# A two-block network on one core: a change to its norms and to one copy in an expert stage

## The chip, the cores and the metric

The kernel runs on one core of one Trainium2 chip, as one launch. The metric is the device time of that launch in microseconds (us). The median of three runs of the kernel before is 4241.9 us; the runs lie from 4215.21 to 4246.16 us.

The engines are named as the profile names them: PE is TensorE (matmuls), PEld its weight loads, DVE is VectorE, ACT is ScalarE, POOL is GpSimd, and SP issues most of the transfers.

## The reference, cut to what matters

A first block (two layers, each a feed-forward net, a mixer of three recurrences, and a second feed-forward net) works on 256 tokens of width 1024. A second block (two layers, attention and an expert stage each) works on the same 256 tokens and on 256 context tokens. What the change touches is the norms, and the expert stage of the second block's first layer.

```python
def rmsnorm(x, w):
    xf = x.astype(jnp.float32)
    y = xf * lax.rsqrt(jnp.mean(xf * xf, axis=-1, keepdims=True) + EPS)
    return (y * w.astype(jnp.float32)).astype(x.dtype)
...
def chunk(args):
    hc, ic, gc = args
    ue = u[ic]
    ve = v[ic]
    act = jax.nn.gelu(jnp.einsum('td,ted->te', hc, ue), approximate=False)
    return jnp.einsum('te,ted->td', gc * act, ve)
```

The kernel computes the expert stage densely: all 16384 experts for every token, times a gate that is zero for the experts that were not chosen.

## The kernel before, in words

**Layout.** Activations stand transposed: channels on the 128 partitions, tokens along the row, so x is a tile of 128 x 8 x 256 (eight channel blocks of 256 tokens). Everything is float32. A matmul of full precision is three matmuls (`mm3`, L242) on operands split into a high and a low part: `split` (L214) takes the high part with an ACT copy (L221) and the low part with a subtraction on DVE (L224), part of it on POOL (L226). `mm` (L239, L240) records every matmul, so all of PE's rows bear L240.

**The order of the work.** No order is written out by hand. The program is traced once, and a planner lays out each engine's queue from a modelled timeline: of the instructions that are ready there, the one traced earliest goes first. On the chip each engine then works through its queue in that order. Tiles of one tag share a fixed number of buffers, and a new tile waits until an old one has been read for the last time.

**The norm.** `quick_rstd` (L299) is the quick form. It squares the eight channel blocks into eight tiles of the tag `g_n`, five on ACT (L308) and three on DVE (L306; blocks 2, 3 and 6). The tag has 4 buffers in the two mixers and in the last expert stage, 5 in the attention of the second block, and 6 in the two closing norms and at the expert stage of the context tokens (`self.gb`, key `n`). `rstd_of` (L288) then sums over the partitions on PE: for every tile of squares, two matmuls with the squares as weights and a column of ones as the moving operand, all into one bank. The trace shows each of them as two matmuls of one column (`pj<-ones,g_n`, or `act<-ones`, `s<-ones`), so 32 for a norm. `rsqrt` (L249) makes the reciprocal root of the 128 x 2 sums on DVE, by an integer guess and three Newton steps, and `spread` (L268) puts it on all partitions with two matmuls by the identity (`pj<-ccom,rsy`). The next work (L328 or L1588) multiplies x with it. Eight norms go this way: one in each mixer, the two closing norms (`scaled_norm`, L1583), one in the attention of x in each layer of the second block, one on the context tokens ahead of the first expert stage, and one ahead of the last expert stage. Eight other norms use `rstd` (L275), which adds its squares on DVE (L284) and hands one tile to `rstd_of`. `rsqrt` has 26 calls in all, 10 of them from norms of heads (`head_rstd`, L312, and L826) on 128 x 8 values.

**The expert stage of the first layer** (`peer_both`, L1528). Groups 0 to 8 run for the context tokens alone (256 tokens, `experts` with `first`), while the gates of x are still being made (`gates`, L1408: DVE makes `g_e` and `g_o`, PE multiplies them into the bank `r`, ACT copies that into `rst` (L1432), and a transfer writes `rst` to the DRAM tensor `gd`). The results stand in four PSUM banks, `acc`. Then groups 9 to 31 run for x and the context tokens together (512 tokens): `hidden` (L1449) loads weights of `u` (into `raw` and `rawx`), splits them (ACT L221) and multiplies; `gated` (L1466) loads the gates (`eG<-gd`, L1469) and multiplies on DVE (L1473), then splits (`eah`, `eal`); `down` (L1478) multiplies by `v` into the banks `acc`, and DVE adds them into the SBUF tile `ef` (L1500). Between the two, ACT copies the four banks of the context tokens into the right half of `ef` (L1556). The first `down` of the 512-token stage needs those banks.

Of the kernel before, what the change touches and what calls it, by code (L numbers as in the profile page):

```python
# [14 lines left out]
I32 = mybir.dt.int32  # L15
# [4 lines left out]
OP = mybir.AluOpType  # L20
# [88 lines left out]
class Net:  # L109
# [42 lines left out]
    def t(self, shape, tag, bufs=1, dt=F32, pool=None):  # L152
        return (pool or self.ph).tile(shape, dt, tag=tag, name=tag, bufs=bufs)
# [95 lines left out]
    def rsqrt(self, ss, n, scale=1.0):  # L249

        nc = self.nc
        c = ss.free_size()
        t = lambda tag, dt=F32: self.t([128, 16], "rs" + tag, 2, dt)[:, 0:c]
        x, xh, a, y = t("x"), t("h"), t("a"), t("y", I32)
        nc.vector.tensor_scalar(x, ss, 1.0 / n, EPS, OP.mult, OP.add)
        nc.vector.tensor_scalar(y, x.bitcast(I32), 1, None, OP.logical_shift_right)
        nc.vector.tensor_scalar_mul(xh, x, -0.5)
        nc.vector.tensor_scalar(y, y, -1.0, float(0x5F3759DF), OP.mult, OP.add)
        y = y.bitcast(F32)
        for _ in range(3):  # L260
            nc.vector.tensor_tensor(a, y, y, OP.mult)
            nc.vector.tensor_tensor(a, a, xh, OP.mult)
            nc.vector.scalar_tensor_tensor(y, a, 1.5, y, OP.add, OP.mult)
        if scale != 1.0:
            nc.vector.tensor_scalar_mul(y, y, scale)
        return y
# [32 lines left out]
    def quick_rstd(self, x):  # L299

        nc = self.nc
        sqs = []
        for k in range(8):
            sqs.append(self.g([128, 256]))
            if k in (2, 3, 6):
                nc.vector.tensor_tensor(sqs[k], x[:, k], x[:, k], OP.mult)  # L306
            else:
                nc.scalar.activation(sqs[k], x[:, k], AF.Square)  # L308
        self.pooled = 2
        return self.rstd_of(sqs)  # L310

    def head_rstd(self, sqs, n, scale, tag):  # L312

# [1118 lines left out]
                    nc.scalar.copy(st.rearrange("p i t -> p t i")[:, t0:t0 + 4], ps)  # L1432
            nc.scalar.dma_start(gd[base + c], st.rearrange("p i t -> p (i t)"))

    def experts(self, h, grps, u_d, v_d, gd, f=None, quiet=()):

        nc = self.nc
        T = h[0].shape[2]  # L1440
        nt = T // 32
        pairs = 512 // T
        gi = pairs
        acc = None
        if T == 256:
            acc = [self.bank((128, 2, 256), "acc") for _ in range(4)]
        acts, G = {}, {}

        def hidden(grp):  # L1449
            self.lead = 0 if T == 512 else LEAD  # L1450
            acts[grp] = []
            for b in range(4):
                if b % 2 == 0:
                    raw = self.raw(u_d[grp * 2 + b // 2])
                W = self.wsplit(raw[:, b % 2 * 1024:(b % 2 + 1) * 1024], [128, 1024])
                if b % pairs == 0:
                    ps = self.bank((128, pairs, T), "act")
                for k in range(8):
                    self.mm3(ps[:, b % pairs], [q[:, k * 128:(k + 1) * 128] for q in W], [q[:, k] for q in h],
                             k == 0 and b % pairs == 0, k == 7 and b % pairs == pairs - 1)  # L1460
                if b % pairs == pairs - 1:
                    a = self.t([128, pairs, nt, 32], "ea", self.na, pool=self.ap_)
                    nc.scalar.activation(a.rearrange("p b c t -> p b (c t)"), ps, AF.Gelu)
                    acts[grp].append(a)

        def gated(grp):  # L1466
            if grp % gi == 0:
                G[0] = self.t([128, nt, 4 * gi, 32], "eG", 2)
                nc.sync.dma_start(G[0], gd.rearrange("c p (i t) -> p c i t", t=32)[:, :, grp * 4:(grp + gi) * 4])  # L1469
            out = []  # L1470
            for n, a in enumerate(acts.pop(grp)):
                for q in range(pairs):
                    nc.vector.tensor_tensor(a[:, q], a[:, q], G[0][:, :, grp % gi * 4 + n * pairs + q], OP.mult)  # L1473
                A = self.split(a.rearrange("p b c t -> p b (c t)"), [128, pairs, T], "ea", 4)
                out += [[z[:, q] for z in A] for q in range(pairs)]
            return out

        def down(grp):  # L1478
            As = gated(grp)
            self.lead = 0 if T == 512 else LEAD  # L1480
            for half in range(2):
                raw = self.raw(v_d[grp * 2 + half])
                if T == 512:
                    banks = [self.bank((128, 512), "acc") for _ in range(4)]
                for b in range(4):
                    if b % 2 == 0:
                        W = self.wsplit(raw[:, b // 2 * 1024:(b // 2 + 1) * 1024], [128, 1024])
                    for m in range(4):
                        o = b % 2 * 512 + m * 128
                        w = [q[:, o:o + 128] for q in W]  # L1490
                        if T == 512:
                            self.mm3(banks[m], w, As[b], b == 0, b == 3)
                        else:
                            mm = half * 4 + m
                            self.mm3(acc[mm // 2][:, mm % 2], w, As[b], grp == grps[0] and b == 0 and mm % 2 == 0,
                                     grp == grps[-1] and b == 3 and mm % 2 == 1)
                if T == 512:
                    for m in range(4):
                        o = f[:, half * 4 + m]
                        nc.vector.tensor_tensor(o, o, banks[m], OP.add)  # L1500

        lag = self.na * pairs // 4 - 1
        for grp in grps:
            self.share = 0 if grp in quiet else 256
            hidden(grp)
            if grp - lag in grps:
                self.xp = self.xp or self.spare
                down(grp - lag)
            yield
        for grp in grps[-lag:] if lag else ():  # L1510
            down(grp)
        self.share, self.lead = 0, LEAD
        return acc
# [14 lines left out]
    def peer_both(self, l, x, ctx, wq_d, keys_d, u_d, v_d, gd, beside):  # L1528

        first, rest = range(0, NFIRST), range(NFIRST, 32)  # L1530
        with self.tc.tile_pool(name="eh", bufs=1, reuse_waits="tile") as hp, self.psum("ex", act=2, acc=4):
            ps, pb = self.ps, self.pb

            def run(gen):
                self.ps, self.pb, self.al, self.ph = ps, pb, {}, hp
                try:
                    while True:
                        yield next(gen)
                except StopIteration as e:
                    self.acc = e.value  # L1540

            self.ap_, self.na, self.ph = hp, 4, hp
            h = (self.t([128, 8, 512], "pH", 1, F32R), self.t([128, 8, 512], "pL", 1, F32R))
            hx, hc = [[q[:, :, j * 256:(j + 1) * 256] for q in h] for j in range(2)]
            self.gb, self.al = dict(n=6), dict(pj="act")
            self.mnorm(ctx, l, 3, 1, hc)
            self.al = {}
            gen = self.experts(hc, first, u_d, v_d, gd[8:16], quiet=range(4, NFIRST))
            next(gen)
            self.route(self.queries(x, l, 0, 2, hx), wq_d, keys_d, gd, 0)  # L1550
            list(run(gen))
            with self.roomy(), self.tc.tile_pool(name="ef", bufs=1, reuse_waits="tile") as fp:
                f = self.t([128, 8, 512], "ef", pool=fp)
                self.nc.gpsimd.memset(f[:, :, 0:256], 0.0)
                for m in range(4):
                    self.nc.scalar.copy(f[:, 2 * m:2 * m + 2, 256:512], self.acc[m])  # L1556
                list(run(self.experts(h, rest, u_d, v_d, gd, f)))
                self.residual(ctx, l, 5, 1, [f[:, 2 * m:2 * m + 2, 256:512] for m in range(4)])
                next(beside)
                for i, _ in enumerate(run(self.experts(hx, first, u_d, v_d, gd[0:8]))):  # L1560
                    if i == 2:
                        list(beside)
                        self.ps, self.pb, self.al, self.ph = ps, pb, {}, hp
                self.residual(x, l, 5, 0, [f[:, 2 * m:2 * m + 2, 0:256] for m in range(4)])
                self.residual(x, l, 5, 0, self.acc)
# [230 lines left out]
```

## Time and profile before

| | |
|---|---|
| median of 3 runs | 4241.9 us (4215.21 to 4246.16) |
| the profiled execution's own time | 4208.75 us |
| its span | 4206.7 us, 76811 instructions |
| mean granted clock of PE | 0.983 |
| PE busy | 4071.0 us (97%) |
| DVE busy | 2822.1 us (67%) |
| ACT busy | 1943.9 us (46%) |
| POOL busy | 1324.3 us (31%) |
| DMA | 727.42 MB, mean 173 GB/s |

The profiled execution is one run of its own: its time is 33 us below the median of the three, and 2 us of it lie outside its span. Every duration read from the trace belongs to it. In a row of the timeline the columns are the start, the duration, the engine, the line, the operation, the tiles written and read, their shapes and the count, and in brackets the idle time of the engine before it with what ended it. A row with a count above one has merged neighbours, and its duration is that of them all.

### The profile page before, as it was taken

Reading aid. Unit: us, or ns where it says so; the run is one execution under the profiler, and the core shown is the slowest. Engines: PE = TensorE matmul, PEld = TensorE weight load, DVE = VectorE, ACT = ScalarE, POOL = GpSimd, SP = SyncE. Lnnn points to the kernel's source line nnn. Section 1 sums busy time; section 2 is a strip of 40 time slices with the busy share of each in tenths; the row PEclk is TensorE's granted clock in tenths of the full one; section 3 lists DMA queues with packets and bytes.
Section 4 is the critical chain, followed back from the end, with each engine's and each line's share of the span. In section 5 each row is a group of like instructions: output and inputs, shape, how many; then the busy total and the mean of one; then the engine's idle time right before and its main releaser. Section 6 shows DMA issues by size and latency. Waiting matters only on the chain.

```text
span 4206.7 us, 76811 instructions
## 1 busy us (share of the span) xinstructions
PE 4071.0 (97%) x31290; PEld 3768.6 (90%) x31290; DVE 2822.1 (67%) x5280; ACT 1943.9 (46%) x2711; POOL 1324.3 (31%) x1239
## 2 busy tenths in 40 slices
PE   8999999999999999999999999999999899899999
PEld 8988999998979987999788888888998699799999
DVE  5686757786869957999444444444656789865555
ACT  4462555545536644566322323232444646544443
POOL 4542444454402201400222222222354130015554
PEclk9999999999999989999999999999999999999999
DMA  5545644545465542466533333433464236676654
GB/s 215 175 175 201 234 172 161 192 152 193 146 226 211 211 169 106 150 219 222 170 120 120 120 120 120 130 111 130 154 212 160 75 139 225 240 276 211 215 196 141
DMA packets 174994, 727.42 MB, mean 173 GB/s; under 512 B 12080, under 2 KB 87088, under 8 KB 103856
## 3 DMA queue, kind: packets, MB, share of 16 engines
q1 hardware_dynamic: 171184, 672.18, 46.1%
q10 hardware_dynamic: 3456, 50.33, 3.1%
q8 instruction: 245, 4.01, 0.4%
q14 instruction: 109, 0.89, 0.1%
HBM read 668.99 MB, written 53.48 MB: 172 GB/s over the span
## 4 chain that ended last, share of the span: by engine, by line
PE 86%; DVE 8%; DMA 2%; ACT 2%; issue 1%; POOL 0%; SPq 0%; DVEq 0%; ACTq 0%; POOLq 0%
PE acc L240 30%; PE act L240 23%; PE pj L240 23%; PE r L240 3%; PE gd L240 2%; DVE wl L224 2%; PE s L240 1%; PE hg L240 1%; PE o L240 1%; DVE g_cv L435 1%; DMA rawm<-wmod 1%; ACT wh L221 1%; PE pt L991 1%; PE at L240 1%; DVE g_o L1422 0%
## 5 line engine op out<-in xcount | busy, mean ns | idle before, releaser
L226 POOL TENSOR_TENSOR wl<-raw,wh 128x256 fp32r<-128x256 f32 (+2 forms) x419 | 537.7, 1284 | 1421.9 <-ACT wh L221 1381.2
L221 ACT CAST wh<-raw 128x1024 fp32r<-128x1024 f32 x592 | 621.7, 1052 | 718.7 <-PE acc L240 324.6
L224 DVE TENSOR_TENSOR wl<-raw,wh 128x768 fp32r<-128x768 f32 (+2 forms) x584 | 620.0, 1063 | 478.1 <-ACT wh L221 472.2
L240 PE MATMUL acc<-eah,wh 128*128 128x256 f32 (+1 forms) x1824 | 557.0, 312 | 15.0 <-ACT eah L221 15.0
L240 PE MATMUL acc<-eal,wh 128*128 128x256 f32 (+1 forms) x1824 | 568.8, 312 | 1.1 <-DVE eal L224 1.1
L240 PE MATMUL acc<-eah,wl 128*128 128x256 f32 (+1 forms) x1824 | 568.1, 312 | 0.0
L240 PE MATMUL pj<-hH,wh 128*128 128x256 f32 x1776 | 501.5, 283 | 15.7 <-ACT wh L221 12.1
L240 PE MATMUL pj<-hL,wh 128*128 128x256 f32 x1776 | 501.4, 282 | 4.1 <-DVE hL L352 2.6
L240 PE MATMUL pj<-hH,wl 128*128 128x256 f32 x1776 | 499.8, 282 | 1.2 <-DVE wl L224 1.2
L240 PEld LDWEIGHTS acc<-eah,wh 128*128 128x128 f32 x1824 | 343.9, 189 | 36.7 <-ACT eah L221 15.2
L240 PEld LDWEIGHTS acc<-eal,wh 128*128 128x128 f32 x1824 | 343.8, 188 | 23.2 <-DVE eal L224 1.8
L240 PE MATMUL act<-pH,wh 128*128 128x512 f32 (+1 forms) x1056 | 358.1, 339 | 5.5 <-ACT wh L221 5.5
L240 PEld LDWEIGHTS acc<-eah,wl 128*128 128x128 f32 x1824 | 343.6, 189 | 21.5
L240 PE MATMUL act<-pL,wh 128*128 128x512 f32 (+1 forms) x1056 | 357.8, 339 | 2.1 <-DVE pL L334 2.1
L240 PE MATMUL act<-pH,wl 128*128 128x512 f32 (+1 forms) x1056 | 357.3, 338 | 0.7 <-DVE wl L224 0.7
L240 PEld LDWEIGHTS pj<-hH,wh 128*128 128x128 f32 x1776 | 337.4, 190 | 21.4 <-ACT wh L221 12.1
L221 ACT CAST wh<-rawx 128x1024 fp32r<-128x1024 f32 x192 | 201.7, 1052 | 325.1 <-PE acc L240 150.2
L240 PEld LDWEIGHTS pj<-hL,wh 128*128 128x128 f32 x1776 | 337.6, 190 | 7.5 <-DVE hL L352 3.5
L224 DVE TENSOR_TENSOR wl<-rawx,wh 128x768 fp32r<-128x768 f32 (+2 forms) x190 | 197.1, 1038 | 215.7 <-ACT wh L221 210.8
L240 PEld LDWEIGHTS pj<-hH,wl 128*128 128x128 f32 x1776 | 337.5, 190 | 3.7 <-DVE wl L224 2.0
L226 POOL TENSOR_TENSOR wl<-rawx,wh 128x256 fp32r<-128x256 f32 (+2 forms) x159 | 217.1, 1366 | 345.8 <-ACT wh L221 333.4
L240 PE MATMUL act<-hL,wh 128*128 128x256 f32 x896 | 252.3, 282 | 0.7 <-DVE hL L334 0.7
(557 smaller groups left out, 11042.3 us busy)
## 6 DMA issues: line engine op xcount, KB each, us to landing
raw<-u SPq DMA_DIRECT2D x114, 1024.0 KB, 4.8
raw<-v SPq DMA_DIRECT2D x104, 1024.0 KB, 4.9
eG<-gd SPq DMA_DIRECT2D x49, 1024.0 KB, 8.5
rawm<-wmod SPq DMA_DIRECT2D x96, 512.0 KB, 5.6
gd<-rst ACTq DMA_DIRECT2D x24, 2048.0 KB, 7.3
raw<-f1gu SPq DMA_DIRECT2D x42, 1024.0 KB, 4.8
raw<-f2gu SPq DMA_DIRECT2D x42, 1024.0 KB, 4.9
rawx<-v SPq DMA_DIRECT2D x42, 1024.0 KB, 4.8
```

Source lines behind the costliest of these rows:

```text
L221: self.nc.scalar.copy(H, src)
L224: self.nc.vector.tensor_tensor(L[..., 0:n], src[..., 0:n], Hf[..., 0:n], OP.subtract)
L226: self.nc.gpsimd.tensor_tensor(L[..., n:], src[..., n:], Hf[..., n:], OP.subtract)
L240: return self.nc.tensor.matmul(out, l, r, start=start, stop=stop)
L435: nc.vector.scalar_tensor_tensor(y[:, j], xp[:, j, i:i + 256], wc(i), y[:, j], OP.mult, OP.add)
L991: nc.tensor.transpose(pt[:, kb % 2, qb * 128:(qb + 1) * 128], P[qb][:, kb * 128:(kb + 1) * 128], self.ident)
```

## The change

Three things are changed. In `rsqrt` the tile `h` (-0.5 x) is no longer made; the factor -0.5 goes into the first product of each Newton step, which is now a `scalar_tensor_tensor`. In `quick_rstd` the squares of blocks 0 to 3 are added into one tile by three DVE additions, and `rstd_of` is given that tile and the squares of blocks 4 to 7. In `peer_both` the four ACT copies of the banks are traced behind `hidden` of the first group of the 512-token stage, not ahead of it.

```diff
@@ rsqrt
-        x, xh, a, y = t("x"), t("h"), t("a"), t("y", I32)
+        x, a, y = t("x"), t("a"), t("y", I32)
         nc.vector.tensor_scalar(x, ss, 1.0 / n, EPS, OP.mult, OP.add)
         nc.vector.tensor_scalar(y, x.bitcast(I32), 1, None, OP.logical_shift_right)
-        nc.vector.tensor_scalar_mul(xh, x, -0.5)
         nc.vector.tensor_scalar(y, y, -1.0, float(0x5F3759DF), OP.mult, OP.add)
         y = y.bitcast(F32)
         for _ in range(3):
-            nc.vector.tensor_tensor(a, y, y, OP.mult)
-            nc.vector.tensor_tensor(a, a, xh, OP.mult)
+            nc.vector.scalar_tensor_tensor(a, y, -0.5, y, OP.mult, OP.mult)
+            nc.vector.tensor_tensor(a, a, x, OP.mult)
             nc.vector.scalar_tensor_tensor(y, a, 1.5, y, OP.add, OP.mult)
@@ quick_rstd
-        return self.rstd_of(sqs)
+        for k in (1, 2, 3):
+            nc.vector.tensor_tensor(sqs[0], sqs[0], sqs[k], OP.add)
+        return self.rstd_of(sqs[:1] + sqs[4:])
@@ experts
-    def experts(self, h, grps, u_d, v_d, gd, f=None, quiet=()):
+    def experts(self, h, grps, u_d, v_d, gd, f=None, quiet=(), begun=None):
...
             hidden(grp)
+            if begun and grp == grps[0]:
+                begun()
             if grp - lag in grps:
@@ peer_both
-                for m in range(4):
-                    self.nc.scalar.copy(f[:, 2 * m:2 * m + 2, 256:512], self.acc[m])
-                list(run(self.experts(h, rest, u_d, v_d, gd, f)))
+                def gather(acc=self.acc):
+                    for m in range(4):
+                        self.nc.scalar.copy(f[:, 2 * m:2 * m + 2, 256:512], acc[m])
+
+                list(run(self.experts(h, rest, u_d, v_d, gd, f, begun=gather)))
```

## Rows read from the trace of the kernel before

**Rows 1.** The page, part 1: busy time and share of the span by engine.

```profile
PE 4071.0 (97%) x31290; PEld 3768.6 (90%) x31290; DVE 2822.1 (67%) x5280; ACT 1943.9 (46%) x2711; POOL 1324.3 (31%) x1239
```

**Rows 2.** The page, part 4: the chain that ended last, by engine.

```profile
PE 86%; DVE 8%; DMA 2%; ACT 2%; issue 1%; POOL 0%; SPq 0%; DVEq 0%; ACTq 0%; POOLq 0%
```

**Rows 3.** Timeline, the last closing norm: start, duration, engine, line, operation, tiles, count.

```profile
4187.73 0.75 DVE L306 TENSOR_TENSOR g_n<-xT 128x256 f32<-128x256 f32 x2
...
4191.60 1.66 DVE L959 SCALAR_TENSOR_TENSOR xT<-acc,mod,xT 128x256 f32<-128x256 f32 x4 [3.11 <-PE acc L240]
...
4192.08 4.18 PE L240 MATMUL pj<-ones,g_n 128*128 128x1 f32 x32
...
4193.37 0.42 ACT L308 ACTIVATE g_n<-xT 128x256 f32<-128x256 f32 x1 [0.45 <-DVE xT L959]
4196.30 0.16 DVE L255 TENSOR_SCALAR rsx<-pj 128x2 f32<-128x2 f32 x1 [2.71 <-PE pj L240]
4196.49 0.17 DVE L256 TENSOR_SCALAR rsy<-rsx 128x2 int32<-128x2 int32 x1
4196.57 0.16 DVE L257 TENSOR_SCALAR rsh<-rsx 128x2 f32<-128x2 f32 x1
4196.70 0.17 DVE L258 TENSOR_SCALAR rsy<-rsy 128x2 int32<-128x2 int32 x1
...
4198.69 1.22 PE L240 MATMUL pj<-ccom,rsy 128*128 128x128 f32 x4 [2.42 <-DVE rsy L263]
```

**Rows 4.** Line L284, additions of squares: durations least, median, most, first and last start.

```profile
L284 DVE TENSOR_TENSOR g_n<-g_n x28: 409/422/951, 454.7 to 3011.5; 128x256 f32<-128x256 f32 x28
```

**Rows 5.** Timeline, the norm of the second mixer.

```profile
994.87 0.75 DVE L306 TENSOR_TENSOR g_n<-xT 128x256 f32<-128x256 f32 x2
995.34 4.09 PE L240 MATMUL pj<-ones,g_n 128*128 128x1 f32 x24 [0.42 <-DVE g_n L306]
995.99 0.43 DVE L306 TENSOR_TENSOR g_n<-xT 128x256 f32<-128x256 f32 x1 [0.36 <-PE pj L240]
```

**Rows 6.** Timeline, PE at the first mixer, the first closing norm, and the attention of x.

```profile
213.22 1.08 PE L240 MATMUL pj<-rawm,sc 128*32 128x256 f32 x8 [3.01 <-DMA rawm<-wmod]
...
1472.80 3.38 PE L240 MATMUL pj<-ones,g_n 128*128 128x1 f32 x29
...
1485.15 4.43 PE L240 MATMUL s<-ones,g_n 128*128 128x1 f32 x20 [0.46 <-DVE g_n L306]
```

**Rows 7.** Timeline, the norm of the second layer's attention.

```profile
3210.89 4.37 PE L240 MATMUL pj<-ones,g_n 128*128 128x1 f32 x24 [0.62 <-DVE g_n L306]
...
3216.13 3.95 POOL L226 TENSOR_TENSOR wl<-rawx,wh 128x1024 fp32r<-128x1024 f32 x2 [8.43 <-DVE rsa L261]
3216.29 1.86 DVE L263 SCALAR_TENSOR_TENSOR rsy<-rsa,rsy 128x2 f32<-128x2 f32 x1
...
3221.85 1.19 PE L240 MATMUL pj<-ccom,rsy 128*128 128x128 f32 x4 [6.59 <-DVE rsy L263]
```

**Rows 8.** Timeline, the start of the 512-token stage.

```profile
2003.04 2.05 ACT L1556 COPY ef<-acc 128x512 f32<-128x512 f32 x4 [0.45 <-ACT rst L1432]
2004.95 1.08 ACT L221 CAST wh<-rawx 128x1024 fp32r<-128x1024 f32 x1
2006.08 0.80 PE L240 MATMUL act<-pH,wh 128*128 128x512 f32 x1 [4.75 <-ACT wh L221]
...
2016.95 1.22 ACT L221 CAST eah<-ea 128x512 fp32r<-128x512 f32 x2 [8.08 <-DVE ea L1473]
```

**Rows 9.** Chain of waits from 1990 to 2030 us: start, duration, what.

```profile
2002.61 6.92 DMA gd<-rst
...
2009.60 6.59 DMA eG<-gd
...
2019.91 10.27 PE acc L240 x44
```

**Rows 10.** Stretch after the wait: busy time by engine, granted clock, DMA share, GB/s.

```profile
2006.00:2010.50 4.50, 4.42 (x10) 3.31 (x11) 2.37 (x2) 2.86 (x4) 4.29 (x4) 0.51 0.49 206
```

## The prediction

> **What bounds the kernel now.** I read the page's busy times first: PE is busy for 97% of the span and no other engine for more than 67% [rows 1]. The chain that ended last is 86% PE [rows 2]. So time is won only where PE stands still and the change ends that wait sooner, and lost wherever it makes PE wait longer. I then went to the places that the change touches. At a norm the timeline shows a strict series: squares on ACT and DVE, small matmuls by the ones column, twelve dependent DVE instructions of `rsqrt`, two matmuls that spread the result [rows 3]. PE has little else there, so most norms lie on the path. At the start of the 512-token stage the chain of waits tells what decides: a write of gates, then their load, then PE [rows 9].
>
> The changes are small beside the run: eight norms of a few us each, and one stall of 4.75 us [rows 8]. About 1% (42 us) is what a measurement of this kernel can tell from no change, its three runs being 31 us apart.
>
> **The small matmuls.** Before, a norm has 32 of them, four for each square; after, 20. At the last norm they take 4.18 us for 32, and when PE runs without a break 3.38 us for 29, so 0.117 us each [rows 3, 6]; in the attention of x 20 take 4.43 us, 0.22 each [rows 6]. Twelve fewer would be 1.4 to 2.6 us for each norm, if PE were always the last to finish. But before, PE works while squares are being made: when the fourth square (block 3) is ready, it has done blocks 0 to 2 and has 20 left. After, it has 20 left too, and starts them only when the third addition is done. So a norm gets later by what the additions take after the fourth square, and gains only what PE was behind then. An addition of this shape takes 0.42 us [rows 4]; with some 0.04 us between dependent instructions (0.16 us ones start 0.20 apart [rows 3]) I count 0.46. Three are 1.4 us, two (where the first pair was free early) 0.9.
>
> Norm by norm:
> - Last closing norm: blocks 2 and 3 are squared by 4188.5, ahead of the last of x, and DVE then idles 3.11 us, so the three additions are free. PE starts at 4192.08 as before. The last square ends at 4193.79; PE works through the sum and blocks 4 to 7 behind their squares, and after the last has block 7's four, half hidden: end near 4194.55, not 4196.26 [rows 3]. Gain 1.7 (1.0 to 1.8), all of it on the end of the run.
> - Second mixer: the fourth square ends at 995.62; three additions bring 997.0. Twenty matmuls at 0.117 to 0.22 end at 999.3 to 1001.4, against 999.43 before [rows 5, 6]. The tag has four buffers here: even before, square 6 waited for PE to free one [rows 5]. After, the first tile stays held until the sum is multiplied, so the later squares come late as well; I take the slow end. Loss 2.0 (0 to 2.4).
> - First mixer: same pattern, but PE's queue waits at this point for modulation weights, 3.01 us from 210.2 to 213.22, and multiplies by them for 1.08 us [rows 6]. A delay of 2.1 moves the sums to 212.3, and `rsqrt` (2.4 us, [rows 3]) then ends at 214.8, 0.5 beyond the cover. Loss 0.6 (0 to 1.0).
> - First closing norm: 29 in an unbroken 3.38 us [rows 6], so PE was a little behind; two to three additions less that. Loss 0.9 (0 to 1.4).
> - Attention of x, first layer: 20 matmuls from 1485.15, the slow pace both before and after [rows 6]. DVE is busy with the norm before it, so two or three additions. Loss 1.0 (0 to 2.0).
> - Context norm ahead of the expert stage and norm of the last expert stage: two additions, 0.9 each (0 to 1.9, and 0 to 2.6 if the pace falls to the slow one).
> - Attention, second layer: the sums move by 1.1. Then `rsqrt` meets POOL's split: while POOL ran 3.95 us, one DVE instruction of two columns took 1.86 us, and PE waited 6.59 us in all [rows 7]. Starting later, fewer instructions are done before POOL begins and more run behind it. Loss 1.0 (0 to 2.4).
>
> Sum of the norms: -1.7+2.0+0.6+0.9+1.0+0.9+0.9+1.0 = +5.6 us (-1.8 to +12.7).
>
> **The Newton steps.** One of thirteen instructions goes, in 26 calls. L257 needs only x and stands in the shadow of L256: L258 follows L256 by 0.21 us, where dependent instructions follow each other by 0.20 [rows 3]. Its removal shortens the chain by some 0.015 us, 0.4 us over 26 calls; at most it gives its own 0.16 us, 4.2 in all, and at least nothing. The fused product replaces one instruction by another of the same two-input kind, so 0. I take -0.4, by the nearest row. The Trainium skill's page "VectorE: DVE Perf Modes" (Rules for kernel authors) says to minimise the count of operations in a chain, since each flushes the pipeline; by that rule the saving would be the 4.2 us, and the spacing in the trace disagrees with it.
>
> **The copies.** They take 2.05 us of ACT, 2003.04 to 2005.09, and the first split of `rawx` stands behind them; PE waited 4.75 us and started at 2006.08 [rows 8]. Moved behind, that split starts about 2 us sooner, if the planner has the weights landed by then, and PE at about 2004.1. But the stage's next step, `down`, waits for the gates: write 2002.61 to 2009.53, load 2009.60 to 2016.20, product, split, and PE from 2019.91 [rows 9]. None of the copies is in this chain. PE would finish its two blocks of `hidden` 2 us sooner and stand still 2 us longer before 2019.9. So 0. Covers: the copies themselves now lie in ACT's 8.08 us of idleness before 2016.95 [rows 8]; put at the very end of it they would hold up `eah` and PE by up to 1.1 us. PE's clock was at half for 4.5 us after the wait (granted 0.51 [rows 10]); if the shorter wait kept it up, those 2.2 us would again be waited out at 2019.91. Bounds -2.1 (the whole move comes through) to +1.1.
>
> **Sum.** +5.6 - 0.4 + 0 = +5.2 us (-8.1 to +13.8). Against the profiled execution (4208.75, of which 4206.7 is span) that is 4214; it lies 33 us under the median, so for the median I add the difference: 4241.9 + 5.2 = 4247.
>
> **Rivals.**
> - *The fewer matmuls and operations pay.* Twelve matmuls off eight norms are 11 to 21 us, Newton 4.2, the copies 2.1: 17 to 27 us, 4215 to 4225. For it: the last norm does behave so. Against: elsewhere PE finishes its early squares before the fourth is ready [rows 5]. Chance 0.14.
> - *The additions collide with POOL* (the slower side). Each is a two-input DVE instruction. If POOL splits weights then, an addition costs 1.86 instead of 0.42 us, as L263 did [rows 7]; the longest of 28 such additions took 0.95 [rows 4]. For all 24 that is 35 us: 4282. It decides from the point where POOL's split starts before the third addition ends. Against: where I see POOL, it starts later (3216.13, when the small matmuls have already ended at 3215.26 [rows 7]). Chance 0.07. The Trainium skill's page "GPSIMD Engine Reference" (Key points) states this sharing, for DVE instructions with two SBUF inputs; the row on L263 agrees.
> - *The planner lays out the queues anew elsewhere.* Other durations in its model can swap a load or a split anywhere, for better or worse; a swap that opens a wait like the 6.59 or 4.75 us ones [rows 7, 8] costs or frees about that much. Eight in one direction make 45 us: 4197 or 4292. Chance 0.08, both signs.
> - *The copies stay where they were*, because in the planner's model the weights land after ACT is free. That changes no time, by the above, and is part of the forecast.
>
> **Chances.** The forecast 0.71, the rivals 0.14, 0.07 and 0.08. Faster by over 1%: half of the third rival, 0.04. Slower by over 1%: the other half and a little of the second, 0.05. Within 1%: 0.91. The range takes the runs' own spread with the bounds of the sum: 4215.2 - 8.1 = 4207 to 4246.2 + 13.8 = 4260; it holds the first rival.
>
> **What would show it.** Twenty small matmuls at each norm, starting after the third addition; at the last norm the sums end near 4194.6 on the old scale; at the second mixer some 2 us later than before. `rsqrt` still takes 2.4 us. ACT splits `rawx` before it copies into `ef`, PE starts about 2 us sooner there, and waits about 2 us for `eal`. I am wrong if norms in the middle get shorter, if the gates' load starts earlier, or if a wait of over 5 us shows up or goes elsewhere.

## The result and the profile after

The changed kernel takes 4256.6 us, median of 17 runs (4247.4 to 4287.5); the kernel before, in 17 runs, 4221.1 (4207.3 to 4254.0). The ratio is 1.0089, 95% interval 1.0071 to 1.0107: 35.5 us slower, within the 1% that was called no change, and clearly not zero. The profiled execution after is 4255.16 us long with a span of 4253.4, 46.7 more than the one before. That one, 4208.75, was a short one of its kernel (median 4221.1), so some 11 of the 46.7 us are no part of the change.

The page of the kernel after, parts 1 and 4, answers to [rows 1, 2]:

```profile
PE 4094.6 (96%) x31194; PEld 3772.8 (89%) x31194; DVE 2829.3 (67%) x5278; ACT 1944.0 (46%) x2711; POOL 1323.6 (31%) x1239
PE 83%; DVE 11%; ACT 2%; DMA 2%; issue 1%; POOL 1%; SPq 0%; ACTq 0%; DVEq 0%; POOLq 0%
```

PE has 96 matmuls fewer (8 norms of 12) and yet is busy for 23.6 us more. DVE's share of the chain has grown from 8% to 11%. So two things happened: PE waits longer for DVE, and PE's own work got slower.

**The norms.** The waits of PE in the kernel after, by what ended them (total us, times, longest):

```profile
PE pj L240 <- DVE rsy L262: 18.4, 7, 6.0
PE pj L240 <- DVE g_n L310: 16.3, 5, 5.3
PE s L240 <- DVE nlam L1071: 7.1, 1, 7.1
PE act L240 <- DVE g_n L310: 3.6, 1, 3.6
```

The second, third and fourth are new: PE stands until the third addition (L310), in the attention of x until the instruction just behind it. They are not all loss, since before PE did the matmuls of the early squares in that time; what each norm lost is summed up further down. The last closing norm, timeline of the kernel after [rows 3]:

```profile
4237.38 0.88 DVE L310 TENSOR_TENSOR g_n<-g_n 128x256 f32<-128x256 f32 x2
4240.24 1.66 DVE L960 SCALAR_TENSOR_TENSOR xT<-acc,mod,xT 128x256 f32<-128x256 f32 x4 [1.98 <-PE acc L240]
...
4240.73 2.62 PE L240 MATMUL pj<-ones,g_n 128*128 128x1 f32 x20
4243.38 0.16 DVE L255 TENSOR_SCALAR rsx<-pj 128x2 f32<-128x2 f32 x1 [1.15 <-PE pj L240]
4245.77 1.22 PE L240 MATMUL pj<-ccom,rsy 128*128 128x128 f32 x4 [2.42 <-DVE rsy L262]
```

The additions end in DVE's idle time. From the start of the last residual products to the end of the sums it is 3.11 us (4240.24 to 4243.35), before 4.66 (4191.60 to 4196.26). `rsqrt` is one instruction shorter, and PE's wait for it is 2.42 us as it was.

The second mixer's norm [rows 5]:

```profile
1002.78 0.75 DVE L305 TENSOR_TENSOR g_n<-xT 128x256 f32<-128x256 f32 x2
1003.45 1.34 DVE L310 TENSOR_TENSOR g_n<-g_n 128x256 f32<-128x256 f32 x3
1004.93 4.40 PE L240 MATMUL pj<-ones,g_n 128*128 128x1 f32 x20 [2.89 <-DVE g_n L310]
```

The fourth square ends at 1003.53 and the sums 5.80 us later; before it was 3.81 us. The norm of the last expert stage:

```profile
3398.20 0.75 DVE L305 TENSOR_TENSOR g_n<-xT 128x256 f32<-128x256 f32 x2
3398.86 1.33 DVE L310 TENSOR_TENSOR g_n<-g_n 128x256 f32<-128x256 f32 x3
...
3400.25 4.34 PE L240 MATMUL pj<-ones,g_n 128*128 128x1 f32 x20 [2.89 <-DVE g_n L310]
...
3406.07 3.95 POOL L226 TENSOR_TENSOR wcl<-rawc,wch 128x1024 fp32r<-128x1024 f32 x2 [8.92 <-ACT wch L221]
3406.21 1.88 DVE L262 SCALAR_TENSOR_TENSOR rsy<-rsa,rsy 128x2 f32<-128x2 f32 x1
3408.12 1.92 DVE L260 SCALAR_TENSOR_TENSOR rsa<-rsy 128x2 f32<-128x2 f32 x1
...
3410.58 1.19 PE L240 MATMUL pj<-ccom,rsy 128*128 128x128 f32 x4 [5.99 <-DVE rsy L262]
```

Here `rsqrt` now runs into POOL's split of the next weights: two instructions of two columns take 1.88 and 1.92 us beside it, and PE waits 5.99 us.

**The 512-token stage.** PE works without a break in it before and after. Two stretches of 200 us (busy time and count of each engine, granted clock, DMA share, GB/s), first of the kernel before, then of the kernel after:

```profile
2100.00:2300.00 200.00, 200.00 (x884) 165.64 (x884) 93.66 (x109) 57.95 (x72) 50.59 (x36) 1.00 0.39 126
2700.00:2900.00 200.00, 200.00 (x884) 165.64 (x884) 95.19 (x111) 61.06 (x77) 53.78 (x38) 1.00 0.38 125
```

```profile
2125.00:2325.00 200.00, 200.00 (x870) 163.33 (x869) 93.55 (x109) 57.89 (x72) 50.55 (x36) 1.00 0.38 123
2725.00:2925.00 200.00, 200.00 (x872) 163.54 (x871) 95.19 (x110) 60.05 (x75) 52.81 (x37) 1.00 0.35 116
```

At the same clock (1.00) and nearly the same DMA share, PE gets through 871 matmuls in place of 884, 1.5% fewer. From its first to its last matmul of 512 columns the stage takes 1009 us (2029.63 to 3038.95), before 995 (2006.08 to 3000.83): 14.5 us more. The 256-token groups of x that follow read the same moving tiles, and they are slower as well; the first 200 us behind the last matmul of 512 columns, before and after:

```profile
3001.20:3201.20 200.00, 199.27 (x1745) 199.08 (x1744) 124.47 (x172) 99.36 (x121) 97.62 (x74) 1.00 0.59 201
```

```profile
3039.30:3239.30 200.00, 199.29 (x1723) 199.09 (x1722) 123.22 (x170) 98.55 (x121) 94.06 (x72) 1.00 0.59 199
```

Their 1711 matmuls take 211.0 us in place of 208.2. Both together are 17 us. By the forms of the 512-token stage's matmuls between 2100 and 2900 us (count, busy us, mean ns of one), three of each kernel, before and after:

```profile
L240 PE MATMUL acc<-eal,wh 128*128 128x512 f32 x446 | 173.5, 389 | 0.0
L240 PE MATMUL act<-pL,wh 128*128 128x512 f32 x434 | 168.8, 389 | 0.0
L240 PE MATMUL act<-pL,wxh 128*128 128x512 f32 x152 | 59.1, 389 | 0.0
```

```profile
L240 PE MATMUL acc<-eal,wh 128*128 128x512 f32 x436 | 171.9, 394 | 0.0
L240 PE MATMUL act<-pL,wh 128*128 128x512 f32 x436 | 169.6, 389 | 0.0
L240 PE MATMUL act<-pL,wxh 128*128 128x512 f32 x144 | 56.8, 394 | 0.0
```

Before, all forms take 389 ns. After, those that multiply `eah` or `eal` by `wh`, and those that multiply `pH` or `pL` by `wxh`, take 394 to 395; `pL` by `wh` is as it was. What tells them apart is where the tiles lie. `rsqrt` no longer allocates its tile `rsh`, two buffers of 64 bytes in each partition, so all tiles allocated behind it lie 128 bytes lower: `eah`, `eal` and `wxh` among them. `pH` and `pL` are allocated ahead of it and `wh` in a pool of its own: they stayed. The slower pairs are those of which one tile moved and the other didn't; the pairs of two moved tiles (`eah` and `eal` by `wxh`), at 391 and 392 ns, lie in between.

**The copies.** ACT and PE at the start of that stage in the kernel after [rows 8]:

```profile
2026.59 2.05 ACT L1560 COPY ef<-acc 128x512 f32<-128x512 f32 x4 [0.45 <-ACT rst L1433]
2028.50 1.08 ACT L221 CAST wh<-rawx 128x1024 fp32r<-128x1024 f32 x1
```

```profile
2029.63 0.79 PE L240 MATMUL act<-pH,wh 128*128 128x512 f32 x1 [4.76 <-ACT wh L221]
```

They stand where they stood, ahead of the split, and PE waits 4.76 us as it did 4.75.

### The profile page after: what moved, and what is told of

It reads as the page before. It is cut to its first block, busy times and chain, and to the rows that moved or that the text cites. A ratio compares the mean times of both kernels' runs of the same rounds, so it can differ in the third digit from the quotient of the medians.

```text
span 4253.4 us, 76604 instructions
## 1 busy us (share of the span) xinstructions
PE 4094.6 (96%) x31194; PEld 3772.8 (89%) x31194; DVE 2829.3 (67%) x5278; ACT 1944.0 (46%) x2711; POOL 1323.6 (31%) x1239
## 4 chain that ended last, share of the span: by engine, by line
PE 83%; DVE 11%; ACT 2%; DMA 2%; issue 1%; POOL 1%; SPq 0%; ACTq 0%; DVEq 0%; POOLq 0%
PE acc L240 29%; PE act L240 24%; PE pj L240 20%; PE r L240 3%; PE gd L240 2%; DVE wl L224 2%; PE s L240 1%; PE hg L240 1%; PE o L240 1%; DVE g_o L1423 1%; DVE g_cv L436 1%; ACT wh L221 1%; POOL gu L382 1%; PE pt L992 1%; PE at L240 1%
## 5 line engine op out<-in xcount | busy, mean ns | idle before, releaser
L226 POOL TENSOR_TENSOR wl<-raw,wh 128x256 fp32r<-128x256 f32 (+2 forms) x419 | 548.6, 1310 | 1424.4 <-ACT wh L221 1389.8
```

The lines of the kernel that those rows point to most:

```text
L226: self.nc.gpsimd.tensor_tensor(L[..., n:], src[..., n:], Hf[..., n:], OP.subtract)
```

## Experiments

"Before" is the kernel before; each median is given beside that of the runs of before that were made with it. The ratio with its 95% interval is the one on record, which is not simply the quotient of the two medians; where the runs lie in two groups (below), the two differ. Spacing is the mean time from the start of one matmul to that of the next. Lines left out of an edit are marked by three dots.

**Each part alone.** First the Newton edit:

```diff
-        x, xh, a, y = t("x"), t("h"), t("a"), t("y", I32)
+        x, a, y = t("x"), t("a"), t("y", I32)
...
-        nc.vector.tensor_scalar_mul(xh, x, -0.5)
...
-            nc.vector.tensor_tensor(a, y, y, OP.mult)
-            nc.vector.tensor_tensor(a, a, xh, OP.mult)
+            nc.vector.scalar_tensor_tensor(a, y, -0.5, y, OP.mult, OP.mult)
+            nc.vector.tensor_tensor(a, a, x, OP.mult)
```

> The kernel before with the Newton edit alone (no rsh tile, -0.5 in the first product); additions and copies as before. Placement theory: 128x512 spacing 230 ns in the 512-token stage, 13 to 17 us more than before, ratio 1.003 to 1.004, although the norms take no longer. Rival (it is the copies or the order): spacing 226.7 ns and 0 to 4 us less than before, as the prediction's term of -0.4 (-4.2 to 0) had it.

Measured: 4239.3 us against 4216.6, ratio 1.0053 (1.0040 to 1.0066), 22.7 us more. One of its six runs took 12105.4 us, for a reason that is not known; the ratio leaves it out, and the median of the other five is 4238.8. Its 512-token stage has the slow pairs, spacing 232 ns for `eah` and `eal` by `wh` and for `pH` and `pL` by `wxh`:

```profile
2150.00:2350.00 200.00, 200.00 (x872) 163.52 (x871) 95.97 (x112) 60.56 (x76) 52.42 (x37) 1.00 0.35 116
```

The edit that was to cost nothing is the largest part of the loss, a little more than placement alone was expected to give.

The additions alone:

```diff
         self.pooled = 2
-        return self.rstd_of(sqs)
+        for k in (1, 2, 3):
+            nc.vector.tensor_tensor(sqs[0], sqs[0], sqs[k], OP.add)
+        return self.rstd_of(sqs[:1] + sqs[4:])
```

> The kernel before with the additions of the squares alone; all tiles lie as before. Placement theory with costlier norms: spacing 226.7 ns in the 512-token stage, 20 to 28 us more than before, all of it at the middle norms and the work around them, ratio 1.005 to 1.0065. The prediction's sum for the norms alone: +5.6 us, ratio 1.0013. Rival (the additions re-lay the queues and slow the 512-token stage too): spacing near 230 ns and 35 to 45 us more.

Measured: 4228.0 against 4216.6, ratio 1.0025 (1.0005 to 1.0045), 11.4 us more, spacing 226.7 ns. That is between the forecast (5.6) and what I had read out of the two traces (20 to 28), which was too much: that reading took in the scatter between executions and what belongs to the Newton edit.

The later copies alone:

```diff
...
-                for m in range(4):
-                    self.nc.scalar.copy(f[:, 2 * m:2 * m + 2, 256:512], self.acc[m])
-                list(run(self.experts(h, rest, u_d, v_d, gd, f)))
...
+                list(run(self.experts(h, rest, u_d, v_d, gd, f, begun=gather)))
```

> The kernel before with the later copies alone. Prediction and placement theory: 0 (-2.1 to +1.1), spacing 226.7 ns, ratio 1.000. Rival (the later copies hold the accumulators and slow the stage): 13 to 17 us more, spacing 230 ns, ratio 1.003 to 1.004.

Measured: 4216.4 against 4216.6, ratio 0.9999 (0.9975 to 1.0022), spacing 226.7 ns: nothing. The three parts make 11.4 + 22.7 - 0.3 = 33.8 us of the 35.5. Each has an interval of several us, so the close agreement is partly chance: what the last expert norm loses beyond that in the profiles with both edits (5.4 us, in the next section) is in none of the parts.

**The changed kernel with the tile kept.**

```diff
-        x, a, y = t("x"), t("a"), t("y", I32)
+        x, _, a, y = t("x"), t("h"), t("a"), t("y", I32)
```

> The changed kernel, with the unused 128x16 tile rsh still allocated in rsqrt, so that every tile allocated behind it lies where it lay in the kernel before. Placement theory (128 bytes of shift slow the matmuls of the 512-token stage): the mean spacing of 128x512 matmuls there falls from 230.0 ns back to 226.7 ns, the stage loses the 17 us, and the time is 15 to 20 us below that of the changed kernel, some 1.004 to 1.006 of the kernel before. Rival (the later copies, or the new order of the queues, slow them): the spacing stays at 230 ns and the ratio stays at 1.009.

> The changed kernel with the rsh tile kept, once more, because its first runs went from 4229 to 4269 us and its profiled run had 117.8 ns for the 128x256 matmuls from 3700 to 4200 us, where all other profiles had 113.3. If that spacing belongs to single runs: 113.3 ns this time in the profile or runs near 4229 us, and a median that is the sum of the single parts, +11 us of the additions, ratio 1.0025 to 1.004. If it belongs to this kernel: 117.8 ns again, and ratio 1.006.

Measured: the 512-token stage is back to 884 and 885 matmuls in 200 us, spacing 226.7 ns for all pairs, so the later copies and the queues' order are out as its cause:

```profile
2150.00:2350.00 200.00, 200.00 (x884) 165.64 (x883) 95.72 (x111) 61.00 (x76) 52.96 (x37) 1.00 0.35 116
```

But the time came back only in part: 4241.5 against 4216.6, ratio 1.0064 (1.0038 to 1.0089), and again 4247.4 against 4217.4, ratio 1.0066 (1.0034 to 1.0099). The runs are spread from 4226.7 to 4272.1. The last stage shows one reason: the same kernel, profiled twice, first and second time:

```profile
3900.00:4100.00 200.00, 200.00 (x1701) 200.00 (x1700) 106.33 (x123) 92.57 (x107) 100.29 (x71) 1.00 0.57 197
```

```profile
3900.00:4100.00 200.00, 200.00 (x1767) 200.00 (x1766) 109.17 (x124) 95.25 (x110) 104.31 (x74) 1.00 0.59 205
```

With equal tiles and clock and nearly equal DMA share the 128x256 matmuls of the last stage ran at a spacing of 117.8 ns in one execution and 113.3 in the other, throughout. That belongs to single executions. The runs of the kernel before fall into two groups: of 35, 26 took 4203 to 4225 us and nine 4235 to 4252, and I call these the lower and the upper group. No execution of before from its upper group was profiled; of the kernels whose 256-column weights keep their place, the three profiled executions with the slow spacing took 4242 to 4261 us and each lies high among its kernel's own runs, so I take the spacing as what divides the groups. My expected ratio of 1.0025 to 1.004 failed; the second profiled execution, whose last stage is at 113.3 ns, took 4236.7 us, and six of the 18 runs less than that, the lowest 4226.7. An estimate accounts for that execution: 4214.9 us (the median of before's lower group) + 11.4 (the additions) + some 5 (the fused product, next experiment) + 5.4 (lost at the last expert norm in the profiles with both edits, next section) = 4237. What my expected ratio had left out are the last two. Why this kernel is in the upper group more often than before is open.

**The Newton instructions without the placement, and the placement without the instructions.** The first is the Newton edit with the same line as above, so that no tile moves.

> The kernel before with the fused -0.5 of the Newton edit, but with the unused rsh tile still allocated, so that no other tile moves. Placement theory: the 22 us of the Newton edit came with the moved tiles, so 0 (-4 to +2), ratio 1.000, spacing 226.7 ns in the 512-token stage. Rival (the edit costs something besides the placement, by moving the start of the 256-column stages, which then keep a slower spacing): the spacing of the 128x256 matmuls between 900 and 985 us is 119 to 120 ns in place of 113.5, and the time is 5 to 12 us more, ratio 1.001 to 1.003.

Measured: 4226.2 against 4217.4, ratio 1.0005 (0.9977 to 1.0033): not to be told from 1, though the medians lie 8.8 us apart, and the interval leaves room for the rival's 5 to 12 us too. The 512-token stage is at 884. The rival's sign is there in the trace. From 905 to 985 us, first the kernel before, then this one:

```profile
905.00:985.00 80.00, 80.00 (x708) 80.00 (x707) 50.50 (x97) 37.62 (x49) 46.37 (x46) 1.00 0.54 190
```

```profile
905.00:985.00 80.00, 80.00 (x669) 80.00 (x669) 53.54 (x147) 34.54 (x47) 43.73 (x51) 1.00 0.47 164
```

5.5% fewer matmuls, 5 us over the 90 us of this stretch (spacing 119.3 to 120.0 in place of 113.5 ns). All five profiles with the fused product have 669 to 671 matmuls there, those of the additions, the copies and the gaps alone 704 to 707. No tile of this kernel lies elsewhere than before, so what sets it is not the placement. That the stage's start decides it, as I had supposed, was not tested; what does is open.

The placement alone:

```diff
             h = (self.t([128, 8, 512], "pH", 1, F32R), self.t([128, 8, 512], "pL", 1, F32R))
+            self.gap(128)
```

> The kernel before with nothing changed but 128 bytes of each partition left empty behind the two moving tiles pH and pL of the 512-token stage's pool; instructions and queues stay as they are. Placement theory: spacing 230 ns in the 512-token stage, acc matmuls with wh weights and act matmuls with wx weights at 232 ns, the other two pairs at 227 to 229 ns, and 13 to 17 us more, ratio 1.003 to 1.004. Rival (the number and order of instructions did it): spacing 226.7 ns and ratio 1.000.

> As the gap of 128 bytes, with 256 bytes left empty. If what counts is how far the weights tile lies from the moving tile modulo 256 bytes: spacing 226.7 ns for all pairs and ratio 1.000. If any move of the tiles from the place they had slows them (their distance in full, or which rows they share): spacing 230 ns and ratio 1.003 to 1.004.

Measured: with 128 bytes 4254.0 against 4217.4, ratio 1.0055 (1.0025 to 1.0085); with 256 bytes 4219.0, ratio 0.9986 (0.9959 to 1.0013). The 512-token stage, first with 128, then with 256 bytes:

```profile
2150.00:2350.00 200.00, 200.00 (x871) 163.32 (x870) 93.96 (x109) 58.24 (x73) 50.59 (x36) 1.00 0.38 122
```

```profile
2150.00:2350.00 200.00, 200.00 (x884) 165.62 (x883) 94.70 (x110) 58.58 (x73) 51.01 (x37) 1.00 0.39 126
```

By the forms, with 128 bytes (2100 to 2900 us), the same pairs are slower by the same 5 ns:

```profile
L240 PE MATMUL act<-pL,wh 128*128 128x512 f32 x440 | 171.2, 389 | 0.0
L240 PE MATMUL acc<-eal,wh 128*128 128x512 f32 x432 | 170.4, 394 | 0.0
L240 PE MATMUL act<-pL,wxh 128*128 128x512 f32 x144 | 56.8, 394 | 0.0
```

With every instruction as before, an empty stretch of 128 bytes costs what the missing tile cost, and one of 256 costs nothing. From first to last matmul of 512 columns the stage takes 1009 us with 128 bytes and 995 with 256; the 1711 matmuls behind it 211.6 and 208.1 us. The median of the first lies higher than 17 us above before because seven of its twelve runs (4253.9 to 4262.9) are in the upper group; the five others are 4230.5 to 4236.9, their median (4233.2) 18 us above that of the lower group of before (4214.9). The profiled runs of both gaps were in the upper group (1669 matmuls from 3900 to 4100 us).

This table sums up where time is lost, in us against the profile of before at the same instruction (median of the differences in start of the DVE and ACT instructions within 15 us of the point). The +13 of the copies, which cost nothing, is the scatter between executions, most of it ahead of 900 and about 1820 us; only the steps are to be read.

| at (us, before) | 900 | 990 | 1460 | 1500 | 1750 | 2020 | 3180 | 3500 |
|---|---|---|---|---|---|---|---|---|
| changed kernel | +4 | +8 | +12 | +16 | +21 | +23 | +40 | +48 |
| additions | +3 | +5 | +7 | +10 | +14 | +18 | +18 | +19 |
| Newton | +10 | +15 | +15 | +15 | +16 | +18 | +35 | +36 |
| Newton, tile kept | +10 | +15 | +19 | +20 | +19 | +25 | +25 | +27 |
| gap of 128 | +4 | +5 | +7 | +7 | +6 | +5 | +22 | +20 |
| changed, tile kept (second) | +8 | +14 | +15 | +20 | +23 | +21 | +21 | +30 |
| copies | +10 | +10 | +8 | +8 | +8 | +13 | +13 | +13 |

**A version that takes the one gain.**

```diff
-    def quick_rstd(self, x):
+    def quick_rstd(self, x, added=False):
...
+        if added:
+            for k in (1, 2, 3):
+                nc.vector.tensor_tensor(sqs[0], sqs[0], sqs[k], OP.add)
+            sqs = sqs[:1] + sqs[4:]
...
-    N.scaled_norm(xT, N.p("final_g"))
+    N.scaled_norm(xT, N.p("final_g"), True)
```

> The kernel before with the three additions in the last closing norm alone, the one place where the forecast saw a gain. Forecast: that norm's matmuls against ones are 20 in place of 32 and end 1.6 to 1.8 us earlier after the residual additions, nothing else moves, and the time is 1.7 us below before, ratio 0.9996, too little to tell from 1. Rival (the norm's end hangs on something else, the late squares of ACT): the same wait, 0 us.

Measured: 4218.4 against 4218.5, ratio 0.9996 (0.9973 to 1.0018). Its last norm:

```profile
4186.64 1.66 DVE L963 SCALAR_TENSOR_TENSOR xT<-acc,mod,xT 128x256 f32<-128x256 f32 x4 [1.98 <-PE acc L240]
...
4189.77 0.16 DVE L255 TENSOR_SCALAR rsx<-pj 128x2 f32<-128x2 f32 x1 [1.14 <-PE pj L240]
```

3.13 us from the residual products to `rsqrt`, before 4.70 [rows 3]: the gain of 1.6 us is there, and too small to be seen in the times.

**The spacing of the 256-column stages.** Can the upper group be avoided? `lead` is the column of its tile at which a split weights block begins: 0 in the 512-token stage, 13 (52 bytes) elsewhere. Three kernels, all with the additions of the last norm alone: the 256-token expert stages at 0, all blocks at 0, the expert stages at 32.

```diff
-            self.lead = 0 if T == 512 else LEAD
+            self.lead = 0
```

> As the additions in the last closing norm alone, and the weights tiles of the 256-token expert stages begin at column 0 as in the 512-token stage, not at column 13 (52 bytes on). If the slower spacings of single runs (117.8 or 120.0 ns for 128x256 in the last stage in place of 113.3, some 28 us) come of that distance of 52 bytes: 113.3 ns in every run, no run 25 us or more above the fastest, and a median of 4213 to 4217. If the distance of 52 bytes is what makes the fast spacing possible: 117 to 120 ns in every run, 4240 or more, ratio 1.006.

> As the additions in the last closing norm alone, and all weights tiles of the kernel begin at column 0. If equal distance modulo 256 bytes is the good one everywhere: 113.3 ns in all 256-column stages, also from 800 to 900 us, where the kernel before has 118, and 3 to 10 us less than with the experts' tiles alone. If the distance of 52 bytes is good where weights are loaded from one tile and the moving tiles from several: slower there, 10 us or more above before.

> As the additions in the last closing norm alone, and the weights tiles of the 256-token expert stages begin at column 32 (128 bytes on) in place of 13 (52 bytes). Column 0 gave 120.0 ns for the 128x256 matmuls of the last stage in the profile and 4261 to 4270 us in all six runs; column 13 gives 113.3 in most runs and 117.8 or 120.0 in some. If the spacing gets better the farther the two tiles lie apart modulo 256 bytes: 113.3 ns in every run, none 25 us above the fastest, median 4213 to 4217, and so a version that beats both. If column 13 is a good place in between: 117 to 120 ns again, 4240 us or more.

Measured: the experts at 0, 4263.8 against 4218.5, ratio 1.0093 (1.0059 to 1.0127), six runs within 4261 and 4270. All at 0, 4318.9, ratio 1.0220 (1.0186 to 1.0254). The experts at 32, 4254.1 against 4217.2, ratio 1.0089 (1.0064 to 1.0115). The last stage with the experts at 0, then at 32:

```profile
3900.00:4100.00 200.00, 200.00 (x1669) 200.00 (x1668) 106.15 (x119) 90.65 (x105) 104.15 (x70) 1.00 0.57 193
```

```profile
3900.00:4100.00 200.00, 200.00 (x1688) 200.00 (x1687) 109.18 (x120) 91.27 (x105) 106.10 (x71) 1.00 0.57 196
```

At column 0 both profiled executions are at 120.0 ns, at 32 the profiled one at 118.6, at 13 most at 113.3. For 512 columns column 0 beats a shift of 128 bytes (the gap); for 256 it is the slowest of the three places tried, and the kernel's 13 the fastest. No version beats the kernel before by a measurable amount.

## Why the prediction was right, and where it was not

The class (within 1%) and the range (4207 to 4260) held; the sum did not. It said +5.2 us (-8.1 to +13.8); the change costs 35.5. The number came within 10 us of the median only because the three runs of before that I added it to (4241.9) were high for that kernel (4221.1). That was luck, and so in part was the class: the interval of the ratio reaches 1.0107.

- **The step that failed: "The Newton steps".** It costed instructions, -0.4 us (-4.2 to 0), and was right on them where it looked: dependent DVE instructions still follow each other by 0.20 us, the removed one stood in a shadow, and the wait for `rsqrt` at the last norm is 2.42 us as before. The Trainium skill's page "VectorE: DVE Perf Modes" (Rules for kernel authors) would have made the chain shorter with each operation; 2.42 against 2.42 us speaks against it here. What the step left out is that the edit also frees a tile. The 128 bytes cost 17 us in the 512-token stage and the 256-token groups behind it (shown by the gaps of 128 and 256 bytes) and the changed instructions some 5 us from 900 to 990 us (seen in five profiles, not to be told from nothing in the times, cause open): together close to the 22.7 us measured.
- **The small matmuls.** +5.6 (-1.8 to +12.7) forecast, 11.4 measured with the additions alone: the mechanism held, the sum came out too small. Last closing norm -1.7 forecast, -1.6 measured. Second mixer +2.0 and +2.0. First mixer +0.6, measured +1.1 with the additions alone (the spread begins at 215.28 us, before at 214.23). First closing norm and attention of x together +1.9, measured +3 to +4: there DVE puts a split of 1.22 us and single squares between the additions. Context norm +0.9, measured about +4 (the table's step from 1500 to 1750 us, which holds other work too). The second layer's attention +1.0, measured +2.2 in the changed kernel and with the additions alone. The last expert norm +0.9 (0 to 2.6): from the fourth square to the spread it takes 5.07 us before, 6.21 with the additions alone (+1.1), and 11.63 in the changed kernel (+6.6), where `rsqrt` meets POOL.
- **The copies.** 0 forecast, -0.3 measured; they didn't even move, the fourth rival, as part of the forecast. The sign that I had named, ACT splitting `rawx` ahead of the copies, did not come, so the zero worked out for copies that do move was not tested. It stood on a near tie: before, PE waits 0.32 us for `eal` when its `hidden` blocks are done; after, it does not wait there, and the chain that ended last runs through the copies and the split.

```profile
2019.91 0.50 PE L240 MATMUL acc<-eal,wh 128*128 128x512 f32 x1 [0.32 <-DVE eal L224]
```

- **"The fewer matmuls and operations pay"** is out: of eight norms one pays.
- **"The additions collide with POOL"** named the right meeting and the wrong instructions. No addition is slowed, 24 of them with least, median and most in ns:

```profile
L310 DVE TENSOR_TENSOR g_n<-g_n x24: 409/420/425, 206.7 to 4237.8; 128x256 f32<-128x256 f32 x24
```

  It is `rsqrt` that slid under POOL's split at the last expert norm (1.88 and 1.92 us for instructions of 0.16). The Trainium skill's page "GPSIMD Engine Reference" (Key points) lets DVE instructions with two SBUF inputs contend with GpSimd; both are such, and agree with it. With the additions alone the same `rsqrt` ends before POOL begins, and PE waits less than half as long:

```profile
3376.12 0.16 DVE L255 TENSOR_SCALAR rsx<-pj 128x2 f32<-128x2 f32 x1 [2.02 <-PE pj L240]
...
3378.59 1.19 PE L240 MATMUL pj<-ccom,rsy 128*128 128x128 f32 x4 [2.51 <-DVE rsy L263]
3379.55 4.25 POOL L226 TENSOR_TENSOR wcl<-rawc,wch 128x1024 fp32r<-128x1024 f32 x2 [8.96 <-ACT wch L221]
```

  POOL starts 7.1 to 7.2 us after the fourth square in both; what differs is when the sums are done. In the changed kernel the twenty small matmuls take 4.34 us at a granted clock of 0.51 (the lower of PE's two levels, 1.2 GHz), with the additions alone 2.39 us at 0.97 (nearly the upper, 2.4 GHz). The stretches of these matmuls, in that order:

```profile
3400.30:3404.60 4.30, 4.29 (x20) 4.20 (x20) 0.36 (x1) 0.42 (x1) 0.00 (x0) 0.51 1.01 427
```

```profile
3373.70:3376.10 2.40, 2.38 (x20) 2.30 (x20) 0.40 (x1) 0.42 (x1) 0.00 (x0) 0.97 1.00 423
```

  PE had stood for 2.89 us ahead of them in both, so that wait alone does not decide it. The forecast had the slow pace as the upper bound of this norm's term, but not that it carries `rsqrt` into POOL's split. Both profiles of the changed kernel with the tile kept show the same (4.18 and 4.22 us for the twenty); whether the two edits together bring it or the single execution does is open.

- **"The planner lays out the queues anew"** came true at most in small: waits of over 5 us show up at the attention of x (7.07), the last expert norm (5.99) and ahead of the second layer's attention (5.34, where before it was 6.59 behind the sums [rows 7]). With the additions alone the first and the third are there too (7.08 and 5.34). I had named such waits as a sign of being wrong; they came at the norms, not at the copies or at the gates' load.

## What to carry to other kernels

An edit that drops or adds a small tile moves every tile allocated behind it: list what moves, and compare the matmul count of an unbroken stretch before and after, since a slower PE shows as a smaller count at full busy time, not as a wait. When a scratch tile goes, keep its bytes as a gap until the gain of the edit itself has been measured. Moving work from PE to another engine pays only where that engine is idle and PE is the last to finish, here at one norm of eight.

## What the runs showed of the hardware

- The spacing of 128x512 f32 matmuls is 226.7 ns where weights tile and moving tile lie as before, or moved by 256 bytes against each other, and 232 ns (224 to 241 for single ones) where they are moved by 128 bytes. The Trainium skill's page "SBUF — State Buffer" (Who interferes with whom) says that PE reads weights and moving operand through independent ports and never waits on anyone; the gap of 128 bytes slows PE by 5 ns a matmul in the pairs named above with no instruction changed, which the second half does not account for. Whether it is a read that waits, no trace here shows.
- The spacing of 128x256 matmuls takes several values that hold for hundreds of microseconds at a granted clock of 1.00: 113.3, 117.8 or 120.0 ns in the last stage. With weights 52 bytes into their tile it differs from execution to execution, with weights at its start it was 120.0 in both profiled executions. What picks the value in an execution was not found.
- After a wait of 2.89 us PE's granted clock in twenty matmuls of one column was 0.51 in one execution and 0.97 in another, and they took 4.34 and 2.39 us.
- Beside a POOL split, single DVE instructions of two columns took 1.88 and 1.92 us in place of 0.16.
